# Making gates and scaled keys where the projection leaves PSUM, and putting small matmuls of the scan side by side

## The chip, the cores and the metric

The kernel runs on one core of a Trainium2 chip. A core has TensorE for matmuls (PE in the profile, its weight loads PEld), VectorE (DVE), ScalarE (ACT), GpSimd (POOL) and SyncE (SP), whose queue issues most DMAs. Each engine works through its own queue in order and waits on semaphores for the others. Data lies in DRAM, in SBUF (128 partitions) and in PSUM, eight banks of 128 x 512 floats that matmuls write. The metric is the device time of one execution in microseconds, the median of several runs.

## The reference

One layer of an encoder trunk on an input of 1024 positions x 1024 channels: two token mixers side by side, a gated merge, then a gated feed-forward network.

```python
proj = jnp.einsum("bsd,de->bse", h, w_in)          # h = RMSNorm(x)
glu_in, q, v, z_f, z_b, og, g_a, g_b = jnp.split(proj, SPLIT_POINTS, axis=-1)
# mixer A: GLU, depthwise convolution over 31 positions, LayerNorm, swish, pointwise
# mixer B, one scan per direction, 8 heads of 128 channels:
f = lb + (1.0 - lb) * jax.nn.sigmoid(zf)
lf = jnp.log(jnp.clip(f, MIN_FORGET, 1.0))
key_gate = (1.0 - lb) * jax.nn.sigmoid(-zf)
# S_t = diag(f_t) S_{t-1} + k_t v_t^T,  o_t = S_t^T q_t,  q = silu(q) * 128 ** -0.5
# x = x + W_out(sigmoid(g_a) * A + sigmoid(g_b) * B); x = x + ffn(RMSNorm(x)); RMSNorm
```

The gate f and the key are made elementwise from the projection's columns z_f and z_b; everything is computed in float32.

## The kernel before

Activations stand with channels on partitions and positions in the free dimension, 128 channels x 512 positions (a "half") to a tile. Float32 products of the dense layers are made from two parts: `split` (L124 to L129) writes a rounded copy `hi` on ACT and the rest `lo = src - hi` on DVE, and `mm3` (L144 to L151) runs three matmuls, hi x hi, hi x lo and lo x hi.

**Projection in pairs.** `pair_job` (L283) takes two tiles of 128 output columns and both halves at once, as a 2 x 2 block product with seven products instead of eight. A product is 12 matmuls. Products run in the order 1, 2, 6, 7, 5, 4, 3 and accumulate in three banks `row`, `b2` and `col`; between them ACT copies partial sums out (`su`, L440), and four results leave: after product 2 (first tile, first half), 5, 4 and 3. The first three are formed by DVE from a bank and a copy (L800); the last is read from `row` directly. `row` and `col` are written again by a later product, so a late `su` copy or a late L800 makes PE wait. Weight parts for the next pair are split while a pair runs: the pages of products 1 and 2 after product 2, the pages of products 6 and 3 after product 3. From the fifteenth pair on, sums of weights for the block product are added by DVE (L298).

The result goes to an `evac` function. `store` (L796) puts it in a page `ev` (three buffers), runs an activation if one is wanted, and stores it in DRAM. Nineteen pairs cover the columns of q and the output gate (pairs 0 to 7), then v, z_f and z_b head by head (`todo`, L810 to L826). The z columns of the last head fall to ordinary jobs (`std_job`) at the start of the next stage. Beside the pairs run the taps of the convolution on DVE (L1039) and, from L1056, LayerNorm over its channels, for each half in turn: the channels are summed on DVE (L1051 to L1053), a matmul with ones spreads the sum (L1065), the mean is taken off (L1067), squares are made on ACT (L1071), summed on DVE, and a matmul with ones sums them over partitions (L611); POOL raises to the power -1/2, ACT spreads the result on a diagonal (L600), a matmul with ones makes it a row for every partition (L601), and ACT copies it (L602). Then the tiles are scaled, shifted and passed through SiLU (L1079), and split for storing.

**The scan.** For each head and half (16 iterations) `scan_inputs` loads q and two z tiles and makes gates `f` and keys `kG` on ACT (L1163 to L1165) with a clamp on DVE (L1166). `scan_base` and `scan_levels` work by doubling: blocks of 1, 2, 4, ... 64 positions. At each level DVE multiplies keys and queries in place by the decays `tb` (`double_keys`, `double_queries`, all through `tt`, L1144), and PE forms the products between neighbouring blocks. Levels up to 16 are taken from interleaved copies (`woven`, L1176) by `level` in matmuls of 32 output rows (L1195): the small levels 0, 1, 2 and 4 in one bank `sc`, levels 8 and 16 in the bank `ob`. Blocks of 32 and 64 come from `blocks` (L1281), into a bank that zero matmuls clear first (L1302). DVE picks from these banks under masks (L1259, L1298). `scan_states` turns the keys (L1320, L1322) and forms the states (L1329); `outputs` of the head before run as `pending`.

`scan_base` is a generator of six steps; `Base.step` runs one. In the main loop, `between` runs after each step of `scan_levels` and `scan_states`, five times an iteration: first some pieces of dense work (the rest of the projection, FILL = 1.77 pieces of 6 matmuls), then one step of the next iteration's base, then one of `pending`.

**What sets the order.** PE follows the program as written (`manual_schedule`, L91). For DVE, ACT, POOL and SP a scheduler sets the order when the program is built, from dependencies and its own estimate of times; `pin` keeps some instructions in program order. Pages come from rings (`tm` four buffers, `ev` three, `kG` three, `f` two, `q` two), and an instruction waits until its buffer is free.

Of the kernel before, what the change touches and what calls it, by code (L numbers as in the profile page):

```python
# [27 lines left out]
GLU_FILL = 2  # L28
GLU_MORE = 4
GLU_LATE = 17  # L30
BASE_STEPS = 1
ALIGN = 128
H = 512
EPS = 1e-6
# [14 lines left out]
def tile_hybrid_encoder(  # L49
# [746 lines left out]
    def store(dst, func=None):  # L796
# [10 lines left out]

        return evac

    todo = [  # L810
        t
        for h in range(NH)
# [175 lines left out]
    V.tensor_tensor(lbw[:, 2, :], lbw[:, 1, :], lbw[:, 1, :], op=ALU.subtract)  # L988
    V.tensor_scalar(lbw[:, 3, :], lbw[:, 2, :], -1.0, 1.0, op0=ALU.mult, op1=ALU.add)

    def lb_of(d, h):
        return lbw[:, 2, d * NH + h : d * NH + h + 1]

# [149 lines left out]
    def tt(o, a, b, op=ALU.mult):  # L1143
        V.tensor_tensor(o, a, b, op=op)  # L1144

    kscale = cp.tile([P, 2 * NH], F32, name="kscale")
    V.tensor_scalar(kscale, lbw[:, 3, :], DK**-0.5, None, op0=ALU.mult)

    def c4(t):
        return t.rearrange("p (c t) -> p c t", c=4)  # L1150

    def scan_inputs(i):


        h, half = divmod(i, 2)
        q = page(hp, "q", 2)
        f = hp.tile([P, 2, H], F32, tag="f", name=nm("f"), bufs=2)
        kG = hp.tile([P, 2, H], F32, tag="kG", name=nm("kG"), bufs=3)
        nc.sync.dma_start(q, d_q[h][half])
        for d in range(2):  # L1160
            z = page(hp, "zi", 3)
            nc.sync.dma_start(z, d_z[d][h][half])
            A.activation(kG[:, d, :], z, AF.Sigmoid, scale=-1.0)  # L1163
            A.activation(z, z, AF.Sigmoid)
            A.activation(f[:, d, :], z, AF.Identity, scale=oml_of(d, h), bias=lb_of(d, h))  # L1165
        V.tensor_scalar(f, f, MIN_FORGET, 1.0, op0=ALU.max, op1=ALU.min)  # L1166
        return q, f, kG, kscale[:, h : h + NH + 1 : NH]

    def pairs(t, h, other=H):

# [46 lines left out]
    def scan_base(ins):  # L1217


        q, f, kG, ks = ins  # L1220
        qF = hp.tile([P, 2, H], F32, tag="qF", name=nm("qF"), bufs=4)
        D_t = hp.tile([P, 4, 32], F32, tag="D", name=nm("D"), bufs=3)
        for d in range(2):
            V.tensor_scalar(kG[:, d, :], kG[:, d, :], ks[:, d : d + 1], None, op0=ALU.mult)
# [45 lines left out]
    def scan_levels(base, S_t, Tt):  # L1270


        qF, kG, tb, D_t, A8, Q8, A16, Q16 = base

        def blocks(b, h):

            for c in range(0, H, P):
                for s0 in range(0, P, h):
                    t0 = s0 ^ h
                    d = s0 // h % 2  # L1280
                    T.matmul(  # L1281
                        b[s0 : s0 + h, c + t0 : c + t0 + h],
                        kG[:, d, c + s0 : c + s0 + h],
                        qF[:, 1 - d, c + t0 : c + t0 + h],
                        start=True,
                        stop=True,
                    )
# [12 lines left out]
        b = bank("sc")  # L1300
        for at, g, _ in each():
            T.matmul(b[g, at : at + 32], none, none, start=True, stop=True)  # L1302
# [135 lines left out]

    NI = 2 * NH
    cur = Base(scan_inputs(0))  # L1440
    ins = scan_inputs(1)
    dense.fill(7)
    for pieces in (3, 4, 4, 3, 0):
        cur.step(1)
        dense.fill(pieces)
    pending = Stream(iter(()))
    for h in range(NH):
        Tt = hp.tile([P, 2, 2, 4], F32, tag="Tt", name=nm("Tt"), bufs=4)
# [3 lines left out]
        for half in range(2):  # L1452
            i = 2 * h + half
            base = cur.result()
            ahead = Base(ins) if i + 1 < NI else None
            ins = scan_inputs(i + 2) if i + 2 < NI else None

            def between(fill):
                dense.fill(fill)
                if ahead is not None:  # L1460
                    ahead.step(BASE_STEPS)
                pending.fill(1)

            S_t = hp.tile([P, 4, P], F32, tag="S", name=nm("S"), bufs=3)
            vl = load(d_v[h][half])
            for n, _ in enumerate(scan_levels(base, S_t, Tt[:, half])):
                if n == 1:
# [5 lines left out]
                between(FILL)  # L1473
            qF, kG = base[:2]
            for _ in scan_states(i, kG, v, Tt, Sf, Sb):
                between(FILL)
            kept.append((S_t, v, qF))
            cur = ahead
        pending = Stream(outputs(h, kept, Tt, Sf, Sb))

    dense.owed = 0
# [549 lines left out]
```

## Time and profile before

| | |
|---|---|
| median of 3 runs | 1738.62 us (1736.96 to 1738.87) |
| the profiled execution | 1740.57 us |
| its span, first to last instruction | 1738.7 us |
| granted TensorE clock | 0.997 |
| DMA, mean | 177 GB/s |
| matmuls | 11806 |

The page gives each engine's busy time in the span. "Idle before, and what ended it" stands at groups and waits: the time in which the engine did nothing ahead of an instruction, and the instruction or DMA whose semaphore released it. In the order of time each row has its start, its duration, the tile it writes and reads, and how many equal instructions it merges. Matmuls are pipelined, so that a row's duration overlaps the next row; the distance of two starts is what PE spends. Windows give the busy time of PE, PEld, DVE, ACT and POOL in a stretch, then granted clock, DMA share and GB/s.

### The profile page before, as it was taken

How to read it: one execution, taken by the hardware profiler on the slowest of the kernel's cores; microseconds unless marked ns; L12 is line 12 of the kernel's file. 1: busy time of each engine (PE TensorE's matmuls, PEld its weight loads, DVE VectorE, ACT ScalarE, POOL GpSimd, SP SyncE). 2: the span in 40 equal slices, each digit the busy share in tenths (PEclk: the TensorE clock that was granted, in tenths of full speed). 3: DMA queues.
4: the chain of work that ended last, by engine and by line, in shares of the span. 5: the costliest groups of instructions: out<-in, count | busy, mean ns of one | idle time of the engine just before them, and what ended most of it. 6: DMA issues, size and time to landing. Idle time of an engine off the chain costs nothing. (4 is left out here: it accounts for less than half of the span.)

```text
span 1738.7 us, 30440 instructions
## 1 busy us (share of the span) xinstructions
PE 1708.0 (98%) x11806; PEld 1408.5 (81%) x11806; DVE 1252.1 (72%) x1919; ACT 828.3 (48%) x1544; POOL 170.1 (10%) x184
## 2 busy tenths in 40 slices
PE   8999999999999999999999999999999999999997
PEld 6878888887888888888878887888887888888775
DVE  4599999746678888788556467676767776657864
ACT  7444433334476777776342245444334434443333
POOL 2211111100000000000000002011111111000110
PEclk9999999999999999999999999999999999999998
DMA  8768888854663444436579466577777876773842
GB/s 285 241 169 186 199 188 194 212 162 157 210 204 108 126 131 126 126 120 200 178 260 326 140 206 194 146 157 153 163 164 166 178 169 152 241 253 113 199 91 97
DMA packets 343750, 308.26 MB, mean 177 GB/s; under 512 B 25262, under 2 KB 255798, under 8 KB 343606
## 3 DMA queue, kind: packets, MB, share of 16 engines
q1 hardware_dynamic: 289590, 267.51, 48.8%
q0 software_dynamic: 44800, 37.76, 15.0%
q10 hardware_dynamic: 9216, 1.05, 0.4%
q8 instruction: 92, 1.51, 0.4%
q14 instruction: 52, 0.43, 0.1%
HBM read 201.40 MB, written 87.03 MB: 166 GB/s over the span
## 5 line engine op out<-in xcount | busy, mean ns | idle before, releaser
L149 PE MATMUL mm<-hx,wp 128*128 128x512 f32 x1068 | 427.6, 400 | 4.9 <-ACT su L440 2.1
L151 PE MATMUL mm<-hx,wp 128*128 128x512 f32 x1068 | 417.7, 391 | 1.0 <-DVE wp L125 0.8
L150 PE MATMUL mm<-hx,wp 128*128 128x512 f32 x1068 | 416.3, 390 | 0.5 <-DVE hx L125 0.5
L125 ACT CAST wp<-wr 128x1024 fp32r<-128x1024 f32 (+2 forms) x147 | 147.2, 1002 | 272.9 <-PE mm L150 108.0
L149 PEld LDWEIGHTS mm<-hx,wp 128*128 128x128 f32 x1068 | 200.6, 188 | 48.3 <-ACT su L440 3.2
L151 PEld LDWEIGHTS mm<-hx,wp 128*128 128x128 f32 x1068 | 200.4, 188 | 47.2 <-DVE wp L125 4.1
L150 PEld LDWEIGHTS mm<-hx,wp 128*128 128x128 f32 x1068 | 200.8, 188 | 40.9 <-DVE hx L125 1.7
L125 DVE TENSOR_TENSOR wp<-wr,wp 128x1024 fp32r<-128x1024 f32 (+2 forms) x145 | 169.2, 1167 | 84.1 <-ACT wp L125 77.7
L1039 DVE SCALAR_TENSOR_TENSOR acc<-gl,v_b,acc 128x1024 f32<-128x1024 f32 x120 | 148.7, 1273 | 0.4
L1144 DVE TENSOR_TENSOR qF<-qF,tb 128x512 f32<-128x512 f32 x96 | 65.0, 685 | 19.9 <-ACT A L1176 19.8
L440 ACT COPY su<-mm 128x512 f32<-128x512 f32 x82 | 47.5, 580 | 51.8 <-PE mm L151 51.7
L149 PE MATMUL tr<-hx,wp 128*128 128x512 f32 x180 | 70.5, 392 | 0.0
L151 PE MATMUL tr<-hx,wp 128*128 128x512 f32 x180 | 70.1, 389 | 0.0
L150 PE MATMUL tr<-hx,wp 128*128 128x512 f32 x180 | 70.0, 389 | 0.0
L1636 DVE SCALAR_TENSOR_TENSOR tm<-gp,v_a,tm 128x512 f32<-128x512 f32 x88 | 65.9, 749 | 3.8 <-ACT tm L1634 2.0
L125 ACT CAST wq<-sw 128x1024 fp32r<-128x1024 f32 x41 | 43.2, 1053 | 53.5 <-PE mm L150 42.6
L1144 DVE TENSOR_TENSOR kG<-kG,tb 128x512 f32<-128x512 f32 x96 | 65.2, 684 | 3.7 <-PE sc L1281 3.6
L149 PE MATMUL mm<-hy,wp 128*128 128x512 f32 x164 | 64.2, 391 | 0.0
L150 PE MATMUL mm<-hy,wp 128*128 128x512 f32 x164 | 63.8, 389 | 0.0
L150 PE MATMUL sc<-hy,wq 128*128 128x512 f32 x164 | 63.8, 389 | 0.0
L151 PE MATMUL mm<-hy,wp 128*128 128x512 f32 x164 | 63.8, 389 | 0.0
L151 PE MATMUL sc<-hy,wq 128*128 128x512 f32 x164 | 63.8, 389 | 0.0
(372 smaller groups left out, 3571.1 us busy)
## 6 DMA issues: line engine op xcount, KB each, us to landing
wr<-in_w_in_dram SPq DMA_DIRECT2D x48, 512.0 KB
wr<-in_ffn_w_up_dram SPq DMA_DIRECT2D x22, 512.0 KB
sw<-in_w_in_dram SPq DMA_DIRECT2D x38, 256.0 KB
d_g<-ft SPq DMA_DIRECT2D x38, 256.0 KB
sw<-in_ffn_w_up_dram SPq DMA_DIRECT2D x38, 256.0 KB
sw<-in_ffn_w_up_dram POOLq DMA_DIRECT2D x19, 512.0 KB, 8.0
wr<-sw POOLq DMA_DIRECT2D x32, 256.0 KB, 3.8
wr<-wr POOLq DMA_DIRECT2D x32, 256.0 KB, 4.2
```

Of the source, the lines that this page charges most:

```text
L125: parts = A.copy(hi, src), eng.tensor_tensor(lo, src, hi.bitcast(F32), op=ALU.subtract)
L149: T.matmul(acc, whi[:, k, :], ahi, start=first, stop=False, skip_group_check=again)
L150: T.matmul(acc, whi[:, k, :], alo, start=False, stop=False, skip_group_check=again)
L151: T.matmul(acc, wlo[:, k, :], ahi, start=False, stop=last, skip_group_check=again)
L440: A.copy(t, acc)
L1039: V.scalar_tensor_tensor(acc, g[:, k : k + S], tap(k), acc, op0=ALU.mult, op1=ALU.add)
L1144: V.tensor_tensor(o, a, b, op=op)
L1636: V.scalar_tensor_tensor(c, g[:, o + k : o + k + H], vec("fdw", k * NF + j), c, op0=ALU.mult, op1=ALU.add,)
```

## The change

A new evacuation `store_gates` takes the place of `store` for the z columns. It makes the key with its scale, and the gate with its clamp, and stores both (`d_k`, `d_f`) instead of z. `scan_inputs` only loads. The scaling of keys in `scan_base` goes. In `scan_levels` the blocks of 32 follow levels 8 and 16 directly, and the blocks of 64 come after two stretches between. The base of an iteration takes its first step one stretch earlier, at the end of the iteration before the last, so that its third step, the small levels, stands directly ahead of the blocks of 64; in `between` the pending outputs now come ahead of the base's step.

```diff
-    d_z = scratch("d_z", 2, NH, 2)
+    d_f = scratch("d_f", 2, NH, 2)
+    d_k = scratch("d_k", 2, NH, 2)
...
+    def store_gates(d, h):
+        def evac(half, x0, x1=None, op=None):
+            f, key = ev(), tmp()
+            if x1 is not None:
+                V.tensor_tensor(f, x0, x1, op=op)
+                x0 = f
+            A.activation(key, x0, AF.Sigmoid, scale=-1.0)
+            A.activation(f, x0, AF.Sigmoid)
+            A.activation(key, key, AF.Copy, scale=kscale_of(d, h))
+            nc.sync.dma_start(d_k[d][h][half], key)
+            A.activation(f, f, AF.Identity, scale=oml_of(d, h), bias=lb_of(d, h))
+            V.tensor_scalar(f, f, MIN_FORGET, 1.0, op0=ALU.max, op1=ALU.min)
+            nc.sync.dma_start(d_f[d][h][half], f)
+
+        return evac
...
-            (OFF_ZF + h * DK, store(d_z[0][h])),
-            (OFF_ZB + h * DK, store(d_z[1][h])),
+            (OFF_ZF + h * DK, store_gates(0, h)),
+            (OFF_ZB + h * DK, store_gates(1, h)),
...
         for d in range(2):
-            z = page(hp, "zi", 3)
-            nc.sync.dma_start(z, d_z[d][h][half])
-            A.activation(kG[:, d, :], z, AF.Sigmoid, scale=-1.0)
-            A.activation(z, z, AF.Sigmoid)
-            A.activation(f[:, d, :], z, AF.Identity, scale=oml_of(d, h), bias=lb_of(d, h))
-        V.tensor_scalar(f, f, MIN_FORGET, 1.0, op0=ALU.max, op1=ALU.min)
-        return q, f, kG, kscale[:, h : h + NH + 1 : NH]
+            nc.sync.dma_start(f[:, d, :], d_f[d][h][half])
+            nc.sync.dma_start(kG[:, d, :], d_k[d][h][half])
+        return q, f, kG
...
-        for d in range(2):
-            V.tensor_scalar(kG[:, d, :], kG[:, d, :], ks[:, d : d + 1], None, op0=ALU.mult)
...
         level(slot(b, 0), A8, row(Q8))
         level(slot(b, 1), A16, row(Q16))
+        S_b = bank("sc")
+        for at, g, _ in each():
+            T.matmul(S_b[g, at : at + 32], none, none, start=True, stop=True)
+        blocks(S_b, 32)
         for n, m in enumerate((m_8, m_16)):
             V.copy_predicated(D_t, over(m), near(slot(b, n)))
-        yield
-        b = bank("sc")
-        for at, g, _ in each():
-            T.matmul(b[g, at : at + 32], none, none, start=True, stop=True)
-        blocks(b, 32)
         tb = double(tb, 32)
         yield
+        yield
+        b = S_b
         blocks(b, 64)
...
-            def between(fill):
-                dense.fill(fill)
-                if ahead is not None:
-                    ahead.step(BASE_STEPS)
+            def between(n):
+                dense.fill(FILL)
                 pending.fill(1)
+                step_of = ahead if n < 4 else following
+                if step_of is not None:
+                    step_of.step(1)
```

The order of PE's queue, in the scan's first iteration, before. `mm` are dense sums, `ob` levels 8 and 16, `sc` the bank of blocks, `tr` the turned v; sizes are those of the output.

```order
L151 MATMUL mm_4640<-hx_4311,wp_4450 128x512
L1195 MATMUL ob_4674<-A_4577,A_4575 32x32 x16
L1195 MATMUL ob_4674<-A_4623,A_4621 32x32 x16
L149 MATMUL mm_4640<-hx_4317,wp_4449 128x512
...
L1302 MATMUL sc_4730<-none 32x32
L1281 MATMUL sc_4730<-qF_4423,kG_4336 32x32 x16
L1470 MATMUL tr_4767<-ident,tm_4672 128x128 x4
...
L1281 MATMUL sc_4730<-qF_4423,kG_4336 64x64 x8
L149 MATMUL mm_4823<-hx_571,wp_4596 128x512
...
L1195 MATMUL sc_4836<-A_4796,A_4794 32x32 x16
L1320 MATMUL tr_4909<-ident,kG_4336 128x128 x4
```

The same place after (line numbers are those of the changed kernel: L1210 is `level`, L1312 the zero matmuls, L1294 `blocks`, L148 to L150 the dense products):

```order
L150 MATMUL mm_4869<-hx_4534,wp_4667 128x512
L1210 MATMUL ob_4909<-A_4800,A_4798 32x32 x16
L1210 MATMUL ob_4909<-A_4852,A_4850 32x32 x16
...
L1312 MATMUL sc_4942<-none 32x32
L1294 MATMUL sc_4942<-qF_4636,kG_4557 32x32 x16
L148 MATMUL mm_4869<-hx_4540,wp_4666 128x512
...
L1210 MATMUL sc_5018<-A_4997,A_4995 32x32 x16
L1294 MATMUL sc_4942<-qF_4636,kG_4557 64x64 x8
L148 MATMUL mm_5116<-hx_603,wp_4825 128x512
```

The dense products between levels 8 and 16 and the zero matmuls are gone from there, and the small levels moved from behind the blocks of 64 to directly ahead of them.

The order of ACT's queue in the projection, at the squares of the LayerNorm's first half, before (`su` are copies out of a pair's banks, `tm` the squares):

```order
L440 COPY su_3667<-mm_3652 128x512
L1071 ACTIVATE tm_3755<-cx_3622 128x512
L125 CAST wp_3699<-wr_3691 128x1024
L1071 ACTIVATE tm_3756<-cx_3622 128x512
L1071 ACTIVATE tm_3757<-cx_3625 128x512
L1071 ACTIVATE tm_3758<-cx_3625 128x512
L440 COPY su_3733<-mm_3652 128x512
L440 COPY su_3747<-sc_3654 128x512
```

And after (L1093 are the squares, L816 to L820 the four activations of `store_gates`, L439 the copies):

```order
L439 COPY su_3823<-mm_3808 128x512
L124 CAST wp_3855<-wr_3847 128x1024
L439 COPY su_3896<-mm_3808 128x512
L816 ACTIVATE tm_3875<-ev_3874 128x512
L1093 ACTIVATE tm_3918<-cx_3771 128x512
L817 ACTIVATE ev_3874<-ev_3874 128x512
L818 ACTIVATE tm_3875<-tm_3875,kscale 128x512
L820 ACTIVATE ev_3874<-ev_3874,lbw 128x512
L439 COPY su_3910<-sc_3810 128x512
L1093 ACTIVATE tm_3919<-cx_3771 128x512
L1093 ACTIVATE tm_3920<-cx_3774 128x512
L1093 ACTIVATE tm_3921<-cx_3774 128x512
```

Three of the four squares moved behind both `su` copies and the activations of a z tile.

DVE's queue at the mean of the same half, before, from the last evacuation of a pair on (`sw` a sum of weights, `wp` a weight split, L1067 the mean taken off). The channel sum (L1053) stands some thirty rows earlier:

```order
L800 TENSOR_TENSOR ev_3634<-sc_3508,su_3581 128x512
L125 TENSOR_TENSOR wq_3562<-w_547_3552,wq_3562 128x512
L298 TENSOR_TENSOR sw_3693<-sw_3693,sw_3696 128x1024
L125 TENSOR_TENSOR wp_3559<-wr_3538,wp_3558 128x1024
L1067 SCALAR_TENSOR_TENSOR cx_3622<-ob_3675,cx_3622 128x512 x2
```

And after (L1073 and L1075 are the channel sum, L821 the clamp of a gate, L1089 the mean taken off):

```order
L1073 TENSOR_TENSOR tm_3832<-cx_3771 128x512
L124 TENSOR_TENSOR wq_3704<-w_563_3694,wq_3704 128x512
L1075 TENSOR_TENSOR tm_3832<-tm_3832,cx_3774 128x512
L297 TENSOR_TENSOR sw_3849<-sw_3849,sw_3852 128x1024
L124 TENSOR_TENSOR wp_3701<-wr_3680,wp_3700 128x1024
L821 TENSOR_SCALAR ev_3783<-ev_3783 128x512
L1075 TENSOR_TENSOR tm_3832<-tm_3832,cx_3774 128x512
L1089 SCALAR_TENSOR_TENSOR cx_3771<-ob_3831,cx_3771 128x512 x2
```

The channel sum moved to directly ahead of its use, its last add behind a weight sum, a split and a clamp.

More of the change, by code (lines that the diff above doesn't have):

```diff
@@ L30 @@
 GLU_LATE = 17
-BASE_STEPS = 1
 ALIGN = 128
@@ L989, in tile_hybrid_encoder, with kscale_of @@
     V.tensor_scalar(lbw[:, 3, :], lbw[:, 2, :], -1.0, 1.0, op0=ALU.mult, op1=ALU.add)
+    kscale = cp.tile([P, 2 * NH], F32, name="kscale")
+    V.tensor_scalar(kscale, lbw[:, 3, :], DK**-0.5, None, op0=ALU.mult)
+    def kscale_of(d, h):
+        return kscale[:, d * NH + h : d * NH + h + 1]
     def lb_of(d, h):
@@ L1144, in tt @@
         V.tensor_tensor(o, a, b, op=op)
-    kscale = cp.tile([P, 2 * NH], F32, name="kscale")
-    V.tensor_scalar(kscale, lbw[:, 3, :], DK**-0.5, None, op0=ALU.mult)
     def c4(t):
@@ L1440, in tile_hybrid_encoder @@
     cur = Base(scan_inputs(0))
-    ins = scan_inputs(1)
+    ahead = Base(scan_inputs(1))
     dense.fill(7)
@@ L1445, in tile_hybrid_encoder @@
         dense.fill(pieces)
+    ahead.step(1)
     pending = Stream(iter(()))
@@ L1454, in tile_hybrid_encoder @@
             base = cur.result()
-            ahead = Base(ins) if i + 1 < NI else None
-            ins = scan_inputs(i + 2) if i + 2 < NI else None
-            def between(fill):
-                dense.fill(fill)
-                if ahead is not None:
-                    ahead.step(BASE_STEPS)
+            following = Base(scan_inputs(i + 2)) if i + 2 < NI else None
+            def between(n):
+                dense.fill(FILL)
                 pending.fill(1)
+                step_of = ahead if n < 4 else following
+                if step_of is not None:
+                    step_of.step(1)
             S_t = hp.tile([P, 4, P], F32, tag="S", name=nm("S"), bufs=3)
@@ L1472, in tile_hybrid_encoder @@
                     A.copy(v.rearrange("p c e -> p (c e)"), b)
-                between(FILL)
+                between(n)
             qF, kG = base[:2]
-            for _ in scan_states(i, kG, v, Tt, Sf, Sb):
-                between(FILL)
+            for n, _ in enumerate(scan_states(i, kG, v, Tt, Sf, Sb)):
+                between(3 + n)
             kept.append((S_t, v, qF))
-            cur = ahead
+            cur, ahead = ahead, following
         pending = Stream(outputs(h, kept, Tt, Sf, Sb))
```

2 lines of the change are left out of this document (1 added, 1 removed).

## The prediction

> **What bounds the kernel now.** I read the page's busy shares first, then the waits of TensorE (PE), then two stretches by windows.
>
> ```profile
> PE 1708.0 (98%) x11806; PEld 1408.5 (81%) x11806; DVE 1252.1 (72%) x1919; ACT 828.3 (48%) x1544; POOL 170.1 (10%) x184
> PE mm L149 <- ACT su L440: 2.9, 3, 1.6
> PE sc L1281 <- DVE qF L1144: 1.9, 2, 1.0
> PE mm L149 <- DVE ev L800: 0.9, 1, 0.9
> PE sc L1329 <- ACT kT L1322: 0.7, 1, 0.7
> 281.80:516.00 234.20, 232.42 (x1204) 189.74 (x1202) 159.67 (x215) 103.25 (x160) 15.23 (x16) 1.00 0.67 196
> 516.00:857.00 341.00, 338.29 (x5521) 284.26 (x5521) 273.76 (x598) 238.89 (x540) 12.83 (x14) 1.00 0.43 133
> ```
>
> PE is busy 98% of the span at full granted clock. In the two stretches that the change touches, the part of the projection that makes v and z (282 to 516 us) and the scan (516 to 857), PE idles 1.8 and 2.7 us. So work taken from ACT or DVE is worth only the waits in the second to fourth of the wait rows. The rest can come only from how PE's own small matmuls stand. But each new wait of PE is paid in full.
>
> **What small matmuls cost PE.** The next rows are PE's order of time in one iteration of the scan; the first column is the start.
>
> ```profile
> 776.28 0.39 PE L150 MATMUL mm<-hx,wp 128*128 128x512 f32 x1
> 776.50 0.39 PE L151 MATMUL mm<-hx,wp 128*128 128x512 f32 x1
> 776.82 0.76 PE L1195 MATMUL ob<-A,A 128*32 128x32 f32 x64
> 777.51 0.50 PE L149 MATMUL mm<-hx,wp 128*128 128x512 f32 x1
> 777.85 0.40 PE L150 MATMUL mm<-hx,wp 128*128 128x512 f32 x1
> ...
> 778.78 0.40 PE L151 MATMUL mm<-hx,wp 128*128 128x512 f32 x1
> 779.10 0.28 PE L1302 MATMUL sc<-none 128*32 128x32 bf16 x16
> 779.22 0.47 PE L1281 MATMUL sc<-qF,kG 128*32 128x32 f32 x32
> ...
> 785.41 0.69 PE L1281 MATMUL sc<-qF,kG 128*64 128x64 f32 x16
> 786.03 0.50 PE L149 MATMUL mm<-hx,wp 128*128 128x512 f32 x1
> ...
> 788.67 0.39 PE L151 MATMUL mm<-hx,wp 128*128 128x512 f32 x1
> 788.99 0.46 PE L1195 MATMUL sc<-q,A 128*32 128x32 f32 x32
> 789.26 1.19 PE L1195 MATMUL sc<-A,A 128*32 128x32 f32 x96
> 790.41 0.46 PE L1370 MATMUL ob<-v,S 128*128 128x128 f32 x2
> ```
>
> Dense matmuls start 0.22 to 0.23 us apart (776.28, 776.50). Into a small group it is 0.32 (776.50 to 776.82): 0.09 more. After it the first dense one takes 0.34 to the next (777.51 to 777.85): 0.11 more. Inside, 64 instructions take 0.69 and 128 take 1.42, 10.8 and 11.1 ns each, so nothing else is fixed. A separate small group costs 0.20 us beside its work. Four stand in an iteration now: levels 8 and 16, blocks of 32, blocks of 64, small levels. After the change two do: 16 joins of the blocks of 32 behind levels 8 and 16, 15 of the small levels ahead of the blocks of 64.
>
> **The sum, gains first.**
>
> A. Blocks of 32 join levels 8 and 16. Both are 32 columns wide, and the zero matmuls between them meet the blocks without a gap (16 of them from 779.10, the blocks at 779.22). 16 x 0.20 = 3.2 us; ends 0 (no gain if the joint costs as much) and 3.2.
>
> B. Small levels (32 columns) meet blocks of 64. No row shows that joint. Ends 0 and 0.20 each; I take half, because the widths differ as they do at a group's edge, though only one of two edges is left: 15 x 0.10 = 1.5.
>
> C. Blocks of 64 wait today for the doubling by 32, 1.9 us in two waits. Afterwards two stretches of dense work and the turning of v stand between, so these go: 1.9.
>
> D. In the projection PE waits 0.9 once for an `ev` that stands behind a weight split in DVE's queue; the order now has it ahead: 0.9. Gains together 7.5.
>
> Work that leaves the scan buys no more:
>
> ```profile
> L1163 ACT ACTIVATE kG<-zi 128x512 f32<-128x512 f32 x32 | 19.4, 635 | 0.2 <-DMA zi<-d_z 0.2
> L1164 ACT ACTIVATE zi<-zi 128x512 f32<-128x512 f32 x32 | 19.4, 632 | 0.0
> L1165 ACT ACTIVATE f<-zi,lbw 128x512 f32<-128x512 f32 x32 | 25.7, 816 | 0.0
> L1582 ACT ACTIVATE xq<-x,v_a 128x512 f32<-128x512 f32 x16 | 11.4, 711 | 0.0
> L1224 DVE TENSOR_SCALAR kG<-kG,kscale 128x512 f32<-128x512 f32 x32 | 15.3, 481 | 17.0 <-ACT kG L1163 17.0
> L1166 DVE TENSOR_SCALAR f<-f 128x1024 f32<-128x1024 f32 x16 | 11.0, 690 | 6.3 <-ACT f L1165 6.2
> ```
>
> ACT loses 19.4 + 19.4 + 25.7 = 64.5 us there and DVE 15.3 + 11.0 = 26.3, all off PE's path. In the projection each of the 32 z tiles now has two sigmoids, a scaled copy (nearest row: `xq`, 711 ns) and the affine step. Each starts some 0.1 us before its forerunner ends, so a chain takes about 0.53 + 0.53 + 0.61 + 0.72 = 2.4 us of ACT, then a clamp on DVE of at most 0.48. 32 stores and 32 loads of 256 KB come on top. Cost 0, with the DMA engines at 0.67 and 0.43: the scan loads have over half an iteration to land. In SP's queue the key's store waits for ACT and the gate's for DVE, with weight loads behind; those are fetched a pair ahead. Without that cover E below grows with each load's delay.
>
> Losses. They lie where the convolution's LayerNorm meets z pairs.
>
> ```profile
> 403.18 1.23 DVE L298 TENSOR_TENSOR sw<-sw,sw 128x1024 f32<-128x1024 f32 x1 [3.31 <-DMA w<-in_w_in_dram]
> 404.32 1.22 DVE L125 TENSOR_TENSOR wp<-wr,wp 128x1024 fp32r<-128x1024 f32 x1
> 405.08 1.02 PE L1065 MATMUL ob<-tm,ones_m 128*128 128x512 f32 x2
> 410.24 0.59 ACT L440 COPY su<-mm 128x512 f32<-128x512 f32 x1 [0.17 <-PE mm L151]
> 414.12 0.94 PE L611 MATMUL ob<-ones_m,tm 128*128 128x1 f32 x8
> 433.95 0.58 ACT L440 COPY su<-mm 128x512 f32<-128x512 f32 x1
> 434.58 0.50 PE L149 MATMUL mm<-hy,wq 128*128 128x512 f32 x1 [0.78 <-ACT su L440]
> 460.86 1.28 ACT L600 ACTIVATE tm<-ident,r 128x128 f32<-128x128 f32 x4 [2.43 <-POOL r L593]
> 463.73 1.05 ACT L125 CAST wp<-wr 128x1024 fp32r<-128x1024 f32 x1 [1.08 <-PE mm L150]
> 464.68 0.58 ACT L805 COPY ev<-mm 128x512 f32<-128x512 f32 x1
> 465.12 1.02 PE L601 MATMUL ob<-tm,ones_m 128*128 128x512 f32 x2
> ```
>
> E. The mean's matmul (405.08) reads a sum whose last add now stands on DVE behind the weight sum, the split and a clamp: 405.45 after the split, 0.4 for the clamp, 0.7 for the add gives 406.55. PE waits 1.5. Ends 0 and 3.3, should the load be that much later.
>
> F. On ACT one square and then a z chain and a second `su` copy stand ahead of the other three squares. From 410.24: copy 0.5, chain 2.4, square 0.5, copy 0.5, three squares 1.6 give 415.7; DVE's last add 0.7 ends at 416.4. The matmul over them was due at 414.12: 2.3. Ends 1.0 and 3.5.
>
> G. At 433.95 an `su` copy came late and PE waited 0.78. Now a table load and a sigmoid stand ahead of that copy.
>
> ```profile
> 487.75 1.28 ACT L1163 ACT_TABLE_LOAD   x1 [2.56 <-DMA zi<-d_z]
> 489.04 1.15 ACT L1163 ACTIVATE kG<-zi 128x512 f32<-128x512 f32 x2
> ```
>
> 1.28 + 0.53 less 0.5, by which the SiLUs can start sooner: 1.3; ends 0 and 1.8. The row has the next activation at once behind the load. The Trainium skill (ScalarE: Activation LUTs, "What ACT_TABLE_LOAD costs") gives 1283 ns and 1380 ns of drain on top, 2.66 us for each switch. With it G would be 2.7, H 1.4 more, and the sum 2.8 later; the row here leaves no room for that drain.
>
> H. In the second half three of the four L600 stand behind the cast that waits for the pair's end, an affine step and the `ev` copy: 464.68 + 0.7 + 0.5 + 3 x 0.32 = 466.84, where PE was due at 465.12: 1.7. With 0.3 for its mean, a fifth of E since no split stands between: 2.0; ends 0 and 3.
>
> I. Where both halves of a pair are z (three pairs), the next pair's `su` copy ends behind a cast (1.0), the rest of one chain (1.3), a chain (2.4) and itself (0.6), 5.3 us; two products of 12 matmuls give it 5.4. 0.2 each, 0.6; ends 0 and 1.5.
>
> J. New waits in the scan, with DVE and ACT emptier than now, when there are three: 0.5; ends 0 and 3. Blocks of 32 need the doubling by 16, which DVE now does half an iteration ahead.
>
> Losses 8.2, gains 7.5: 0.7 later. The profiled execution took 1740.57 us and its span 1738.7; it stands 2 us above the median of 1738.62, to which I add: 1739.3.
>
> **The rivals.** Faster: E, F and H don't come, since DVE and ACT reach these rows sooner than I reckon. Then 2.4 of loss stands against 7.5: 1733.5. For it speaks that PE will itself be later at each by what it lost at the one before; against it, the order of both queues is fixed. It decides once over half of the 8.2 fails to come.
>
> Slower, joints that pay nothing, so the change doesn't do what it says: gains 2.8, 1744.0. For it: no row shows levels next to blocks; against it, zeros and blocks of 32 meet freely. Decides when a join gives under 0.05 us.
>
> Slower, the `su` copies come late at every pair with z, not only in I: the copy's margin in a mixed pair is 5.4 less 4.0. DVE, which still runs convolution taps in the first of these pairs, would have to hold each `ev` back by 1.4 us. 14 copies, 0.5 each: 1739.3 - 0.6 + 7.0 = 1745.7. Against: those taps leave after the first pairs.
>
> The drain by the Trainium skill's page would give 1742.1, at the bound.
>
> **Numbers.** About 0.2%, 3.5 us, is what a measurement of this kernel can tell from no change. Chances: forecast (within 0.2%) 0.40; faster 0.26; joints 0.14; late copies 0.16; drain 0.04, which with its own spread I count as slower. So faster 0.26, same 0.40, slower 0.34. The forecast's own range is 1735.2 to 1742; the whole, 1731.5 to 1747.5, takes in the rivals and the bounds of A, B and J.
>
> **What would show it.** A, B: two small groups an iteration instead of four, dense spacing disturbed twice, a joint from levels to zeros without gap. C: no wait at the blocks of 64. E to H: PE waits of 1.5, 2.3, about 2 and 1.7 us around 405, 415, 434 and 466. I: short waits for an `su` copy at the start of the pair that follows two z tiles. Wrong if the LayerNorm rows show no waits, or if the scan is not some 6 us shorter.

## The result, and the profile after

The changed kernel takes 1746.95 us, the median of five runs (1746.53 to 1750.39), beside 1738.62 us of the kernel before (1736.96 to 1741.96): ratio 1.0048, 95% interval 1.0035 to 1.0062. It is slower by 0.5%. The profiled execution took 1746.95 us, its span 1745.2, 6.5 more than that of before.

The first two rows are windows of the kernel before, the next two of the changed kernel. Each pair covers the same matmuls: the pairs that make v and z, then the scan. The columns are the stretch, its length, the busy times of PE, PEld, DVE, ACT and POOL, and then the granted clock, the DMA share and GB/s.

```profile
298.30:495.90 197.60, 195.82 (x861) 159.89 (x860) 123.93 (x156) 82.27 (x125) 12.76 (x14) 1.00 0.66 196
514.40:848.70 334.30, 331.59 (x5493) 278.45 (x5479) 269.37 (x592) 238.40 (x539) 12.83 (x14) 1.00 0.42 131
```

```profile
298.50:518.60 220.10, 203.50 (x862) 162.90 (x861) 136.16 (x184) 140.27 (x218) 12.83 (x14) 0.98 0.70 210
537.00:861.00 324.00, 323.70 (x5494) 278.81 (x5482) 255.27 (x555) 190.61 (x461) 12.88 (x14) 1.00 0.51 160
```

The projection lost 22.5 us, the scan gained 10.3. What is left, some 5 us gained after the scan, lies in a stage whose order on ACT is that of before; its time differed by -5.3 to +6.1 us over the profiles below, with and without the change, so nothing is put down to it. The table of stages further down measures all kernels between the same matmuls.

PE's waits in the changed kernel from 282 to 530 us, the stretch that lost:

```profile
PE mm L148 <- ACT su L439: 6.5, 4, 3.1
PE mm L148 <- ACT hx L124: 3.2, 2, 2.4
PE ob L611 <- DVE tm L1075: 2.8, 1, 2.8
PE ob L601 <- ACT tm L600: 1.8, 1, 1.8
PE mm L149 <- DVE hx L124: 1.4, 3, 1.0
PE ob L1087 <- DVE tm L1075: 0.9, 1, 0.9
```

These are 16.6 us where the kernel before has 1.7. With the half clock below, the two explain 19.2 of the 22.4 us that the table of stages puts on the projection. The rest stands beside the waits, since the profile counts a wait from the modelled end of the matmul before it: at 333.83 it shows 3.1 us, and from start to start PE lost 3.3 there and 0.1 more at the next matmul. Lines below the changed functions have moved: L148 to L150 are the dense matmuls, L439 the `su` copy, L816 to L821 the chain of a z tile. Inside the scan, where before's matmuls waited 1.9 us for the doubling and 0.7 for the turned keys, one row is left:

```profile
PE mm L149 <- issue: 0.3, 1, 0.3
```

**The first z pairs.** The next rows are the order of time at 302 us; at a row's end stands how long its engine was idle, and what ended that.

```profile
302.11 0.86 POOL L301 DMA_DIRECT2D wr<-wr  x1 [7.09 <-DMA wr<-sw]
307.45 1.05 ACT L124 CAST wp<-wr 128x1024 fp32r<-128x1024 f32 x1 [4.95 <-DMA wr<-wr]
308.40 0.60 ACT L816 ACTIVATE tm<-mm 128x512 f32<-128x512 f32 x1
308.89 0.59 ACT L817 ACTIVATE ev<-mm 128x512 f32<-128x512 f32 x1
309.37 0.72 ACT L818 ACTIVATE tm<-tm,kscale 128x512 f32<-128x512 f32 x1
309.98 0.81 ACT L820 ACTIVATE ev<-ev,lbw 128x512 f32<-128x512 f32 x1
310.69 0.58 ACT L439 COPY su<-mm 128x512 f32<-128x512 f32 x1
311.32 0.50 PE L148 MATMUL mm<-hy,wp 128*128 128x512 f32 x1 [1.32 <-ACT su L439]
```

Weight sums of these pairs are still made by accumulating DMAs that POOL issues. ACT's queue has a cast of such a sum ahead of the chain and of the `su` copy. The DMA landed so late that ACT stood 4.95 us; then the chain's 2.3 us came on top, and the copy missed PE by 1.3. At 330 the same happened with more in the queue, and PE waited 3.1.

**The LayerNorm's squares.** The chain stands among the squares, as its order had it:

```profile
415.83 0.59 ACT L439 COPY su<-mm 128x512 f32<-128x512 f32 x1 [1.91 <-PE mm L150]
416.85 0.62 ACT L1093 ACTIVATE tm<-cx 128x512 f32<-128x512 f32 x1
...
419.21 0.57 ACT L439 COPY su<-sc 128x512 f32<-128x512 f32 x1
419.68 1.15 ACT L1093 ACTIVATE tm<-cx 128x512 f32<-128x512 f32 x2
421.06 0.63 ACT L1093 ACTIVATE tm<-cx 128x512 f32<-128x512 f32 x1 [0.24 <-DVE tm L1073]
```

Between the first square (416.85) and the others stand the rest of a chain and a second `su` copy; PE waited 2.8 us for the sum over them.

**The start of the scan's stage.** SP's queue, ACT and PE at 502 us, where the second half of h is loaded into pages of the ring `tm` and split for the dense matmuls:

```profile
501.29 0.32 SPq L819 DMA_DIRECT2D d_k<-tm  x1
502.82 4.88 SPq L117 DMA_DIRECT2D tm<-d_h  x2
506.01 1.26 ACT L124 CAST hx<-tm 128x512 fp32r<-128x512 f32 x2 [4.04 <-DMA tm<-d_h]
506.68 0.51 PE L148 MATMUL mm<-hx,wp 128*128 128x512 f32 x1 [2.43 <-ACT hx L124]
```

Two loads of h stand in SP's queue behind the stores of a key and a gate, and the key's page is one of the four of `tm`. By the starts of its matmuls PE lost some 6 us from 504 to 512; 4.6 of them are the waits for `hx` in the list above.

**The clock.** Windows of the changed kernel just after three of these losses:

```profile
334.60:338.20 3.60, 3.60 (x10) 2.82 (x9) 2.10 (x3) 0.13 (x1) 0.90 (x1) 0.53 1.30 252
424.10:426.90 2.80, 2.80 (x8) 2.15 (x7) 0.36 (x1) 1.44 (x4) 1.24 (x2) 0.50 0.00 0
512.80:515.70 2.90, 2.90 (x8) 2.22 (x8) 2.74 (x6) 1.28 (x2) 0.00 (x0) 0.50 0.97 297
```

The granted clock falls to half, and dense matmuls start 0.427 us apart in the place of 0.227. The three places cost 1.6, 1.5 and 1.2 us beside the waits themselves.

**The scan.** One iteration, PE in order of time:

```profile
727.17 0.39 PE L150 MATMUL mm<-hx,wp 128*128 128x512 f32 x1
727.49 0.75 PE L1210 MATMUL ob<-A,A 128*32 128x32 f32 x63
...
728.26 0.46 PE L1294 MATMUL sc<-qF,kG 128*32 128x32 f32 x32
728.64 0.49 PE L148 MATMUL mm<-hx,wp 128*128 128x512 f32 x1
...
735.21 0.46 PE L1210 MATMUL sc<-q,A 128*32 128x32 f32 x32
735.49 1.07 PE L1210 MATMUL sc<-A,A 128*32 128x32 f32 x96
736.49 0.69 PE L1294 MATMUL sc<-qF,kG 128*64 128x64 f32 x16
737.11 0.50 PE L148 MATMUL mm<-hx,wp 128*128 128x512 f32 x1
```

Two small groups, as meant. By the medians of the starts over all iterations, the first join saves 0.135 us (levels, blocks of 32 and the edges around them and v's transposes: 1.841 before, 1.706 after), the second 0.22 (2.55 before, 2.33 after): 2.2 and 3.3 us in all. The first of four transposes that had stood behind a small group took 0.165 us to the next, and 0.109 now; with the outputs' products that is another 1.8 us. The waits that went are 2.6 us, and 0.1 to 0.3 more at other groups. Together 10 of the 10.3.

### The profile page after: what moved, and what is told of

It reads as the page before. It is cut to its first block, busy times and chain, and to the rows that moved or that the text cites. A ratio compares the mean times of both kernels' runs of the same rounds, so it can differ in the third digit from the quotient of the medians.

```text
span 1745.2 us, 30583 instructions
## 1 busy us (share of the span) xinstructions
PE 1705.8 (98%) x11806; PEld 1411.7 (81%) x11806; DVE 1247.1 (71%) x1903; ACT 844.8 (48%) x1569; POOL 170.1 (10%) x184
## 5 line engine op out<-in xcount | busy, mean ns | idle before, releaser
L148 PE MATMUL mm<-hx,wp 128*128 128x512 f32 x1068 | 427.6, 400 | 4.9 <-ACT hx L124 3.5
L150 PE MATMUL mm<-hx,wp 128*128 128x512 f32 x1068 | 417.8, 391 | 1.1 <-DVE wp L124 1.1
L148 PEld LDWEIGHTS mm<-hx,wp 128*128 128x128 f32 x1068 | 201.0, 188 | 47.8 <-ACT hx L124 4.7
L150 PEld LDWEIGHTS mm<-hx,wp 128*128 128x128 f32 x1068 | 200.9, 188 | 46.0 <-DVE wp L124 3.2
L148 PE MATMUL tr<-hx,wp 128*128 128x512 f32 x180 | 70.5, 392 | 0.0
L439 ACT COPY su<-mm 128x512 f32<-128x512 f32 x82 | 47.5, 579 | 47.4 <-PE mm L150 46.9
L150 PE MATMUL tr<-hx,wp 128*128 128x512 f32 x180 | 70.0, 389 | 0.0
L148 PE MATMUL mm<-hy,wp 128*128 128x512 f32 x164 | 65.1, 397 | 4.5 <-ACT su L439 4.5
L150 PE MATMUL mm<-hy,wp 128*128 128x512 f32 x164 | 64.5, 393 | 0.0
L148 PE MATMUL sc<-hy,wq 128*128 128x512 f32 x164 | 63.8, 389 | 0.0
```

The source lines that it names most:

```text
L148: T.matmul(acc, whi[:, k, :], ahi, start=first, stop=False, skip_group_check=again)
L150: T.matmul(acc, wlo[:, k, :], ahi, start=False, stop=last, skip_group_check=again)
L439: A.copy(t, acc)
```

## The experiments

The first four runs had to divide the loss and the gain between the two halves of the change.

**The scan's order alone.** From the changed kernel, the gates go back into the scan:

```diff
-            (OFF_ZF + h * DK, store_gates(0, h)),
-            (OFF_ZB + h * DK, store_gates(1, h)),
+            (OFF_ZF + h * DK, store(d_z[0][h])),
+            (OFF_ZB + h * DK, store(d_z[1][h])),
...
-            nc.sync.dma_start(f[:, d, :], d_f[d][h][half])
-            nc.sync.dma_start(kG[:, d, :], d_k[d][h][half])
+            z = page(hp, "zi", 3)
+            nc.sync.dma_start(z, d_z[d][h][half])
+            A.activation(kG[:, d, :], z, AF.Sigmoid, scale=-1.0)
+            A.activation(z, z, AF.Sigmoid)
+            A.activation(f[:, d, :], z, AF.Identity, scale=oml_of(d, h), bias=lb_of(d, h))
```

> The scan's new order alone: z is stored and gates and keys are made in the scan, as before. Theory one (the two traces: the scan is 10.3 us shorter by its matmuls alone, the loss lies all where z leaves PSUM): 1738.6 - 10.3 = 1728.3, 1725.5 to 1731. Theory two (the scan got shorter because ACT and DVE were relieved of the gates; with them back its waits, some 3 us, come back): 1731.3 or more. The forecast's own prices (A 3.2, B 1.5, C 1.9, new waits 0.5): 1732.5. In the trace under theory one: no wait of PE of 0.9 us or more inside the scan, two small groups an iteration, no wait for su copies beyond before's.

Measured: 1745.72 us beside 1741.84 of the kernel before, taken together with it, ratio 1.0024 (1.0008 to 1.0040). Theory one fell, and the forecast's prices with it. The groups of matmuls are as short as in the changed kernel, but PE waits inside the scan again. Its waits there, and DVE's longest one:

```profile
PE tr L1323 <- DVE kG L1149: 4.6, 2, 2.5
PE sc L1197 <- ACT A L1178: 1.8, 2, 1.5
PE sc L1332 <- ACT kT L1325: 0.9, 2, 0.5
```

```profile
DVE kG L1226 <- ACT kG L1165: 22.1, 12, 4.0
```

7.3 us of waits, smaller ones of 0.2 to 0.3 and six matmuls at half clock behind the longest eat the joins' gain. The scan is 0.5 us longer than before's.

**The gates alone.** From the kernel before, `store_gates` and the loads are put in as in the change, the scan's order stays.

```diff
-            (OFF_ZF + h * DK, store(d_z[0][h])),
-            (OFF_ZB + h * DK, store(d_z[1][h])),
+            (OFF_ZF + h * DK, store_gates(0, h)),
+            (OFF_ZB + h * DK, store_gates(1, h)),
```

> Gates and keys are made and stored where z leaves PSUM; the scan only loads, but keeps the order of before. Theory one: the 22.6 us that the projection lost come, nothing is gained: 1738.6 + 22.6 = 1761, and at least 1756 should some 5 us after the scan be gained with it. Theory two (relief of ACT and DVE shortens the scan by its three waits, 2.8 us): 1753 to 1758. The forecast's prices (losses E to I 7.7, ev wait gained 0.9): 1745.4.

Measured: 1764.08 us, ratio 1.0127 (1.0109 to 1.0145), 22.2 us more than before: theory one. The projection is 26.1 us longer, the scan as long as before's to 0.1 us, with 2.9 us of waits for the doubling. So relief of ACT and DVE alone buys nothing in the scan, the new order alone buys nothing either, and together they give 10 us.

**The key in pages of its own at the scan's start.** From the changed kernel:

```diff
-            f, key = ev(), tmp()
+            f, key = ev(), key_page[0]()
...
+    key_page[0] = lambda: page(hp, "ky", 2)
```

> The changed kernel; only the z columns of the last head, made at the start of the scan's stage, put the key in two pages of their own instead of the ring tm. Theory one (the loads of h stood behind keys in the ring tm; PE lost 6.1 us in waits from 504 to 512 and 1.2 us at half clock behind them): 1746.95 - 7.3 = 1739.7, 1738 to 1742, with no wait for hx of over 0.5 us there. Rival (the loads are late because SP's queue waits for the key's and gate's stores, or the DMA engines are full): under 2 us gained, 1745 or more, and the waits stay.

Measured: ratio 1.0063 (1.0045 to 1.0081), nothing gained beside 1.0060, which the changed kernel had when it was measured again. In the profile the stretch from 504 to 516 is 2.9 us shorter than in the changed kernel's first profile, not 7.3, and 0.8 us shorter than in its second, which has the same pages of `tm`. One key from the last pair still held a page of `tm`, and SP's queue still had the two loads behind a key's and a gate's store. At 330 that execution waited 4.8 us for the `su` copy. So the theory isn't borne out, and what the ring is worth apart from the queue is not shown.

**No store of keys.** From the changed kernel:

```diff
-            nc.sync.dma_start(d_k[d][h][half], key)
...
-            nc.sync.dma_start(kG[:, d, :], d_k[d][h][half])
+            nc.sync.dma_start(kG[:, d, :], d_f[d][h][half])
```

> The changed kernel without the store of the keys (the scan loads the gate in their place, so that its loads stay): ACT's chain is whole, but each z tile has one store as before. Theory one (32 more stores delay the weight sums that POOL's queue makes by DMA; the cast that waits for them holds up chain and su copies on ACT): the waits at 309 and 330, 4.8 us, and 1.6 us at half clock behind them go, and with the key's page free at once also the 7.3 us at 504: 1746.95 - 13.7 = 1733.3, 1731 to 1736; the waits at the LayerNorm's sums (3.0, 1.0, 2.0 us) stay. Rival (ACT's chain by itself makes the su copies late): the waits at 309 and 330 stay, 1739.7.

This kernel leaves the keys out: its scan reads the gate in their place, so that its output is not the layer's and only its times are of use.

Measured: 1742.43 us, ratio 1.0006 (0.9992 to 1.0019), some 9 us below the changed kernel's ratio of 1.006, where theory one had 13.7. The projection is 9.4 us shorter than in the changed kernel's first profile (8.1 than in its second), and still 13.0 longer than before's. At 330 ACT reached the cast 3.2 us earlier, and the `su` copy was nearly in time:

```profile
325.42 1.04 ACT L124 CAST wp<-wr 128x1024 fp32r<-128x1024 f32 x1
...
329.97 0.56 ACT L439 COPY su<-mm 128x512 f32<-128x512 f32 x1
```

At 309 a wait of 0.9 us stayed. The LayerNorm's 2.8 and 1.8 stayed to the tenth, as they should if the queues' order makes them; the mean's 0.9 fell to 0.3. So of 22.4 us, 13 come with the chain alone and 9.4 only with the second store and the page that it holds: 4.9 of them up to 340, 4.1 after 500 (3.7 and 2.0 by the changed kernel's second profile). What makes the weight sums late stays open: here they still took 3.3 to 7.4 us to land, with fewer bytes moved than before.

The next four asked what the store does by itself, whether a shorter chain would do, and what the changed kernel takes on the chip of these runs.

**Two stores, old chain.** From the kernel before:

```diff
             nc.sync.dma_start(dst[half], t)
+            if also is not None:
+                nc.sync.dma_start(also[half], t)
```

> The kernel before with one more store of each z tile, from the same page to DRAM that nobody reads; ACT's work is as before. Theory one (it takes both, later weight sums by more DMA traffic and ACT's long chain behind the cast that waits for them): weight sums land later than before's 3.3 to 5.3 us, but no wait for su copies over 0.6 us at 300 to 340, ratio 1.000 to 1.002. Rival (the traffic alone makes the copies late): waits of 1.3 and 3.1 us there as in the changed kernel, with the half clock 6 us, ratio 1.003 or more.

Measured: 1743.19 us beside 1742.51, ratio 1.0000 (0.9986 to 1.0014): theory one. Weight sums took 3.3 to 6.7 us to land, before's 3.3 to 5.3, the changed kernel's 5.2 to 8.3. The cast is then 0.6 us later than before's, and with one copy between, the `su` copy has time to spare:

```profile
305.93 1.06 ACT L125 CAST wp<-wr 128x1024 fp32r<-128x1024 f32 x1 [3.25 <-PE mm L150]
306.88 0.58 ACT L806 COPY ev<-mm 128x512 f32<-128x512 f32 x1
308.88 0.59 ACT L440 COPY su<-mm 128x512 f32<-128x512 f32 x1 [1.41 <-PE mm L151]
```

32 more stores alone are free, as the prediction had it. It takes the chain with them.

**One sigmoid outside, with the new order and with the old.** `store(d_z[d][h], AF.Sigmoid)` for z; in the scan

```diff
-            A.activation(kG[:, d, :], z, AF.Sigmoid, scale=-1.0)
-            A.activation(z, z, AF.Sigmoid)
+            V.tensor_scalar(
+                kG[:, d, :], z, kminus[:, n : n + 1], kscale[:, n : n + 1], op0=ALU.mult, op1=ALU.add
+            )
             A.activation(f[:, d, :], z, AF.Identity, scale=oml_of(d, h), bias=lb_of(d, h))
```

> The scan's new order; of the gates only one sigmoid(z) is made where z leaves PSUM (by the activation that copies there now, for the other results one of 0.63 us more), one store as before; in the scan DVE makes the key from it (in the place of its scaling) and ACT the affine step, so ACT loses four sigmoids an iteration, 38.8 us. Theory one (the new order pays once ACT and DVE reach the scan's small matmuls in time, and the projection loses only by long chains and more stores): the scan 8 to 10 us shorter than before's, the projection 1 to 4 us longer: 4 to 9 us less than the kernel before, ratio 0.995 to 0.998. Theory two (only the whole relief makes the order pay): waits for keys and interleaved copies stay in the scan, ratio 1.000 or more.

> The same gates (one sigmoid where z leaves PSUM, the rest in the scan) with the scan's old order. Theory one: the relief alone buys at most the scan's three waits of before, 2.8 us, and the projection loses 1 to 4 us: ratio 0.999 to 1.002. Theory two (the relief itself shortens the scan, the order does not matter): as fast as the one with the new order, within 2 us.

Measured: ratio 0.9996 (0.9981 to 1.0012) with the new order, 1.0074 (1.0051 to 1.0098) with the old. With the new order the scan is 7.2 us shorter than before's, near what theory one said, but the projection loses 7.5, more than its 1 to 4: even one activation more for three of four z tiles, with the table loads that the LayerNorm's SiLUs then force, makes `su` copies late (3.4 us of waits, 0.9 in the kernel with two stores) and results of DVE (4.0, there 2.0). With the old order the scan is 8.3 us longer than before's, which neither theory had. Its matmuls for the blocks of 64 wait 7.4 us in five waits for the doubling by 32, where before waited 1.9, and 2.6 us at half clock stand behind them:

```profile
PE sc L1283 <- DVE qF L1144: 7.4, 5, 3.0
```

The scheduler's order on DVE moved, and the old place of these blocks has no slack for it. In the new order two stretches of dense work stand there, and the wait doesn't exist in any of its profiles but one (0.2 us).

**The changed kernel again.** No edit.

> The changed kernel again, beside the others of this call, so that they stand against it on one chip: ratio 1.003 to 1.007 by its first runs. The waits at 309 and 330 hang on when DMAs land and may differ by some us between executions; those at the LayerNorm's sums (2.8, 1.8, 0.9) hang on the order of queues and should come back within 0.2.

Measured: 1754.37 us beside 1742.51, ratio 1.0060 (1.0039 to 1.0082). The waits at the LayerNorm's sums came back at 2.8, 1.8 and 0.9 us; the `su` copies at 309 and 330 were worth 0.8 and 2.5 us in the place of 1.3 and 3.1.

By now all was said for gates in the scan, where the projection is left alone, if they could be there in time. The last runs keep z stored and the new order.

**Inputs one iteration earlier.**

```diff
+    ins = scan_inputs(2)
...
-            following = Base(scan_inputs(i + 2)) if i + 2 < NI else None
+            following = Base(ins) if i + 2 < NI else None
+            ins = scan_inputs(i + 3) if i + 3 < NI else None
```

The ring of `kG` gets a fourth buffer for it.

> The scan's new order with z stored and all gates made in the scan, but q and z are loaded and gates made one iteration earlier (four buffers of kG in the place of three). Theory one (with gates in the scan the new order fails because keys come too late: the first step of a base now stands one stretch earlier, its inputs do not; DVE waited 22 us in 12 waits for kG there): the waits for kG and A in the scan, 6.4 us, go; the scan is 7 to 10 us shorter than before's, ratio 0.995 to 0.997. Theory two (ACT carries 64.5 us too much for the new order): the waits stay, ratio 1.000 to 1.003 as with the inputs where they were.

**One sigmoid a tile in the scan.** As the edit with the sigmoid outside, but z is stored, and `A.activation(z, z, AF.Sigmoid)` stands in the scan.

> The scan's new order with z stored; in the scan ACT makes one sigmoid a tile in the place of two, DVE makes the key from it (in the place of its scaling), so ACT has 20 us less and nothing else moves. Theory two (ACT's load): the scan 3 to 6 us shorter than before's, half way to the 7.2 us that the run with the sigmoid made outside showed: ratio 0.9965 to 0.9985. Theory one (the inputs' lead): waits for kG stay, ratio 1.000 to 1.003.

**Both.**

> Both: one sigmoid a tile on ACT, and inputs one iteration earlier; the projection is that of before. By either theory the best of the set: the scan 8 to 10 us shorter, the projection within 2 us of before's: ratio 0.994 to 0.9965, some 6 to 10 us below the kernel before and 14 to 18 below the changed one. It falls if the earlier loads collide with the jobs at the scan's start, where SP's queue and the ring tm were late in the changed kernel.

Measured: ratios 1.0001 (0.9989 to 1.0013), 0.9983 (0.9971 to 0.9995) and 0.9975 (0.9964 to 0.9987). With the inputs earlier the waits stay for the most part, as theory two had it, but not because ACT is late with what is needed next: it makes each key one iteration sooner (the first of the seventh iteration ends at 577.7 us, at 597.6 with the scan's order alone). The key's scaling on DVE moved with it, and there it still stands ahead of doublings of the iterations before and waits for ACT:

```profile
DVE kG L1226 <- ACT kG L1165: 16.7, 11, 3.7
583.05 0.49 DVE L1226 TENSOR_SCALAR kG<-kG,kscale 128x512 f32<-128x512 f32 x1 [3.49 <-ACT kG L1165]
```

PE keeps 6.0 us of waits, where the scan's order alone had 7.3 and the smaller ones; the scan is 2.7 us shorter than before's. With 20 us less on ACT the scan is 4.4 us shorter than before's, with both 5.8. The last is the fastest kernel of the study, 0.25% below the kernel before (1737.75 beside 1742.10, taken together), less than the 6 to 10 us expected. Its scan, by the windows' columns, and the one kind of wait left there:

```profile
517.20:845.70 328.50, 324.87 (x5497) 278.89 (x5485) 271.30 (x595) 218.22 (x509) 13.53 (x14) 1.00 0.44 134
PE tr L1326 <- DVE kG L1151: 3.5, 3, 1.3
```

**Keys on POOL.** From that kernel, `G.tensor_scalar` in the place of `V.tensor_scalar` for the key.

> The fastest of the runs so far (z stored, new order, one sigmoid a tile in the scan, inputs one iteration earlier) with the 32 keys made on POOL in the place of DVE, which takes 15 us off DVE. Theory (what is left of the scan's waits, 3.5 us in three for kG ahead of its transposes, is DVE's queue, which in the changed kernel has the keys and the clamp less): the three waits go, the scan comes from 5.8 to 8 to 10 us shorter than before's, ratio 0.9955 to 0.997. Rival (POOL makes a key slower than its place allows, or slows DVE beside it): new waits for kG in the first step of a base, ratio 0.9975 or more.

Measured: ratio 1.0033 (1.0019 to 1.0047): the rival. A key takes POOL 1.43 us on the mean (1.21 in the median, 3.98 at most) where DVE takes 0.54, the scan is 4.0 us longer than before's, and the waits for kG ahead of the transposes grew to 5.1 us.

```profile
L1169 POOL TENSOR_SCALAR kG<-zi,kminus,kscale 128x512 f32<-128x512 f32 x32 | 45.4, 1427 | 241.9 <-PE mm L1326 178.4 <-DVE A L1151 23.0 <-ACT A L1183 20.8
```

The stages of all profiles, as differences in us from the kernel before. The stages part at the starts of the same four matmuls by number in PE's order (1300, 2422, 7892 and the last of 11806).

| kernel | to 298 | v and z, to 514 | scan, to 849 | the rest |
|---|---|---|---|---|
| changed | 0.2 | 22.4 | -10.3 | -5.3 |
| changed, again | 2.9 | 21.1 | -9.7 | 3.0 |
| key in its own pages | 0.5 | 23.8 | -10.8 | -2.5 |
| no store of keys | 0.3 | 13.0 | -10.1 | -4.1 |
| gates alone | 0.7 | 26.1 | 0.0 | 0.1 |
| scan's order alone | 2.8 | 2.1 | 0.5 | -2.2 |
| two stores | 0.4 | 1.5 | 0.5 | 0.2 |
| one sigmoid outside, new order | -0.8 | 7.5 | -7.2 | 2.3 |
| one sigmoid outside, old order | 1.9 | 6.2 | 8.3 | 6.1 |
| inputs earlier | 2.1 | 4.6 | -2.7 | -2.7 |
| one sigmoid in the scan | 1.6 | 1.4 | -4.4 | 3.1 |
| both | 0.7 | 2.2 | -5.8 | -2.5 |
| keys on POOL | 1.8 | 2.6 | 4.0 | -4.8 |

The first and the last column, where these kernels do the same work, show what one profile can differ by: some 3 us in the first, 6 in the last. The middle columns are read against waits, not alone.

## Why the prediction was right or wrong

The time lies inside the range and just under its upper end, and in part by luck: the first profile of the changed kernel gained 5.3 us after the scan, where ACT does the same work in the same order, and lost 3.0 there in its second. Measured again, the kernel stood at 1.0060 times the one before, which on 1738.62 makes 1749.1, above the range. The likeliest case, no change at 1739.3, was wrong: both sums were too small, the losses by far more than the gains.

- **A, the first join: 3.2 forecast, 2.2 measured.** The blocks of 32 stood ahead of v's transposes, not of dense work, so one of their two edges was already cheap (0.127 us). The transposes behind a small group had a price of their own, which was not seen: 0.9 us came back there.
- **B, the second join: 1.5 forecast, 3.3 measured**, a little above its upper end. Small levels and blocks of 64 meet in 0.126 us, and the 128 small matmuls ahead of it span 0.11 us less, since a stall among them (0.05 to 0.15 us in most iterations before) went. The rival that the joints pay nothing fell.
- **C, waits of the blocks of 64: 1.9 forecast, 1.9 measured**, and 0.7 for the turned keys went with it. The run with one sigmoid and the old order shows that this wait hangs on DVE's order and can be 7.4 us.
- **D, the wait for `ev`: 0.9 forecast and gone** (the changed kernel was 0.9 ahead at 304 us).
- **"Work that leaves the scan buys no more" was wrong.** It is right for the old order (the gates alone leave the scan as long as it was). But the new order pays only with that work gone: with the gates back in the scan its 10 us shrink to nothing. The prediction priced the two halves as if they added.
- **The stores "at cost 0" were wrong**, and this is the largest error. The two stores alone are free. With the chain the second store costs 9.4 us (8.1 by the changed kernel's second profile), most of it where `su` copies stand behind a cast that waits for a weight sum (309 and 330) and where the loads of h are late (504). The working looked at weight loads in SP's queue and at the scan's loads; it missed the loads of h, and the sums that arrive by POOL's queue. It missed the ring `tm` too, in which the key takes a page; what that page alone costs is not shown.
- **The half clock was not in the sum**: 4.3 us in three places.
- **E, the mean's matmul: 1.5 forecast, 0.2 measured** (0.6 in the second profile). PE itself came later, as the faster rival had it; here it was right.
- **F, the squares: 2.3 forecast, 2.8 measured**, and 1.5 at half clock behind it. **G, the `su` copy behind a table load: 1.3 forecast, 0.7 more than before measured.** **H, the second half: 2.0 forecast, 2.7 measured** (0.9 at the mean, 1.8 at L601). **I, pairs of two z tiles: 0.6 forecast, one wait of 0.5** (5.3 us against 5.4, as it was worked out, gave no wait; the 0.2 each was an allowance). The orders of ACT's and DVE's queues told these to a microsecond.
- **J, new waits in the scan: 0.5 forecast, 0.3 measured.**
- **The rivals.** Late `su` copies (1745.7) came nearest in time, and they were late, but by another mechanism than the one named: not DVE holding back `ev`, but a cast ahead of the chain, waiting for a DMA; and only in two of the 14 places. The drain behind table loads fell: the load at 443.11 took 1.28 us and began 0.02 us after the instruction before it, and the sigmoid started 1.29 us after the load's start. The Trainium skill (ScalarE: Activation LUTs, "What ACT_TABLE_LOAD costs") gives 1380 ns more; this trace disagrees.

In sum the projection was forecast to lose 6.8 (E to I, less D) and the scan to gain 6.1 (A to C, less J); they lost 22.4 and gained 10.3.

## What to carry to other kernels

Two edits of which neither shortens a stage alone can take 10 us off it together, and a sum of terms won't tell: ask of each edit what the other needs to be in time. Where an engine works through one queue in order, a longer chain is priced at the latest arrival ahead of it, so look for the instruction in that queue that waits for a DMA, and for every load that will stand behind a new store. On a kernel with PE at 98% the stage that has no slack is the worst place for work that another stage hides: leaving the gates in the scan and cutting ACT's work there (one sigmoid for two) beat both kernels.

## What the runs showed that was not expected

A wait of PE is dearer than its length. Over the fourteen profiles there are 17 waits of 2.1 us or more between 250 and 900 us, by the profile's idle times, and 15 of them were followed, 2.6 to 5.3 us after they began, by 3 to 12 dense matmuls at 0.427 us apart, half the clock: 0.6 to 2.4 us more. Of 64 waits from 0.8 to 2.1 us only five were.

Where a wait lies counts as well as its length. In the clock's records of these profiles the stretches at half clock last 3.41 or 6.83 us, and within one profile their starts lie whole multiples of 3.413 us apart (334.84, 423.59 and 512.33 in the changed kernel, twice 26 of them). On this grid, and by the same idle times, in the nine profiles that have such a stretch between 250 and 900 us, PE idled 1.9 us or more in 16 windows, and the next window ran at half clock after each; after windows with 0.8 to 1.8 us it did so 6 times in 50. The two long waits that cost nothing more by themselves, 2.4 and 2.9 us, lay across two windows. The Trainium skill (TensorE: Matmul & The Clock Gate, Part 1) has the two states of the clock, and one idle window of about 3.4 us as what brings the slow one; here 2.1 us of waiting was enough.

Work on POOL was slower than its neighbour's by more than a factor of two: the same key, 128x512 with two scalars, took 1.43 us on the mean there and 0.54 on DVE.
